# Attention with negated scores and one q stack for two heads; part of the weights' sums moved from attention into the recurrence and the gate units

## The chip, the cores and the metric

The kernel runs on one core of a Trainium2 chip. The metric is the device time of one execution in microseconds (us). Engines are named as in the profile: PE is TensorE (matmuls and transposes; PEld is its weight load), DVE is VectorE, ACT is ScalarE, POOL is GpSimd, SP is SyncE, which here issues nearly all DMAs.

## The reference

One layer of a streaming encoder: 1024 tokens, 1024 features, float32. With h = RMSNorm(x):

```
z = h @ w_in                      # q, f, i, g of the recurrence; q, k, v of attention; two gates
oa = hgrn2_mixer(...)             # 4 heads of 128, gated linear recurrence, chunks of 64
ob = band_attention(q, k, v, ...) # 8 heads of 64; a chunk of 64 sees itself and 8 chunks before it
x = x + (sigmoid(gate_a) * (oa @ w_branch_a) + sigmoid(gate_b) * (ob @ w_branch_b)) @ w_out
x = x + (silu(h2 @ w_gate) * (h2 @ w_up)) @ w_down          # h2 = RMSNorm(x), 2816 wide
x = x + sigmoid(h3 @ w_ple_gate) * (p @ w_ple_proj)         # h3 = RMSNorm(x)
```

The part that the change touches most is the band attention:

```
qh, kh = head_rms(q, qn_g), head_rms(k, kn_g)   # t * rsqrt(mean(t*t over the head) + 1e-6) * gain
scores = qh @ kh.T / 8 + rel_bias[clipped distance]   # -1e30 outside the band
o = softmax(scores) @ v
```

## The kernel before

**Matmuls.** Every matmul of weights is made of three: each operand is split into a rounded part hi and a rest lo, and hi*hi, hi*lo and lo*hi are summed in PSUM. The hi of a weight is cast by ACT (line 123) and its rest lo is subtracted by POOL, sometimes DVE (line 126). Weights pass through `weights()`: load by SP into `raw` (2 buffers), cast, rest, into a ring of 4, up to three units ahead of use. Large products (w_out, the gates, the feed-forward) use Strassen's scheme with 7 products in place of 8; the sums of weight blocks that it needs are S1 to S4.

**Who sets the order.** `Pinned` and `order()` chain PE's matmuls, SP's DMAs and the operations called through `self.V`, `self.A` and `self.G` in the order of the program text; their line in the profile is 54, since the helper records them. Other operations are placed by the framework's scheduler. The program is written as generators ("streams") that yield after a piece of PE work; `weave` interleaves two of them by their planned PE time, `drain` runs one to its end.

**Stages.** `first_norm` loads x and starts the first products. `hgrn_in(h)` projects head h of the recurrence; its inner part `near(h)` prepares products. `hgrn_mix(h)` runs the recurrence of a head by levels m = 1, 2, 4 .. 64: at each level DVE multiplies halves of q and kt (SBUF operands), PE makes the scores, and DVE puts them into place with `copy_predicated` under 0/1 `masks` (32-bit words, levels below 32). `hgrn_in(h+1)` is woven with `hgrn_mix(h)`, and `attn_v` with the last mix. Then come `attention()`, `gate_units()`, `branches()`, `out_proj()`, the feed-forward and the last part.

**Attention.** 32 steps, each one pair of heads and one block of 128 queries. `attn_in` (a feed taken piece by piece) makes q and k of four heads at a time; for the head norm ACT squares, DVE sums over 64, and POOL takes the power -1/2 (line 556) and multiplies by the token's factor r (line 557); `r64` = r*r/64 is made once on DVE (lines 526, 527). `attn_stack` transposes q and k of a pair into PSUM; ACT copies them with their gains into k1 and `qs` (two tiles of 128 columns), DVE makes the rests k2 and the lower half of qs. `attn_scores` multiplies, and one DVE operation per part adds the bias and keeps a running maximum; DVE negates the maximum, ACT takes exp with it as bias, and DVE or ACT divides by the row's sum (head 1: DVE's TENSOR_SCALAR over the row). `attn_pt` transposes the probabilities and copies them into `pt`, `attn_pv` multiplies with v.

**The weights' sums.** S1 to S4 of w_out (4 jobs) and of w_down (11 jobs) are worked out by POOL from the raw weights and spilled to DRAM until their stage. `quad_slow` does this: per job two loads of 512 KB, four POOL operations of 128x512 (lines 1069, 1073, 1075, 1080) and four stores, in four slots of the large pool. 12 jobs (`QUADS`) run beside attention, two stream steps for each of its yields, and the other 3 in `gate_units`, one step for each of the five later yields of `strassen_weights`, in all units but the last.

Of the kernel before, what the change touches and what calls it, by code (L numbers as in the profile page):

```python
# [9 lines left out]

F32 = mybir.dt.float32
F32R = mybir.dt.float32r
U32 = mybir.dt.uint32
AF = mybir.ActivationFunctionType
ALU = mybir.AluOpType
AX = mybir.AxisListType

P = 128
# [3 lines left out]
HALF = 512  # L22
# [9 lines left out]
RAW = 2  # L32
AHEAD = 3
PLAIN = 4
QUADS = 12


C_MIX, C_FFN, C_PLE, C_ON, C_GQ, C_GK, C_LB = 0, 8, 16, 24, 25, 26, 27
# [3 lines left out]
def f32(ap):  # L42
    return ap.bitcast(F32)
# [13 lines left out]
class Trunk:  # L57
# [150 lines left out]
    def norm_sums(self):  # L208

        nc = self.nc  # L210
        ps = self.mm()
        for b in range(8):
            self.mul(ps[:, b:b + 1], self.acc[:, b * P:b * P + P], self.ones[:, 0:1], start=True, stop=True)
        v = self.small(8)
        nc.vector.tensor_scalar(v, ps[:, 0:8], 1.0 / D, EPS, ALU.mult, ALU.add)
        self.r = self.small(8, tag="rtok")
        nc.gpsimd.tensor_tensor(self.r, v, self.mhalf[:, 0:8], ALU.pow)

    def norm_rows(self):

# [300 lines left out]
    def attn_in(self):  # L521

        nc = self.nc
        late = []
        self.r64 = self.small(8, tag="r64")
        nc.vector.tensor_tensor(self.r64, self.r, self.r, ALU.mult)
        nc.vector.tensor_scalar(self.r64, self.r64, 1.0 / 64, None, ALU.mult)

        def scale():
            two, b, ps, ss = late.pop(0)  # L530
            for i in range(2):
                qk = self.small(HALF, tag="qk")
                self.V.tensor_tensor(
                    qk[:, :].rearrange("p (a two d) -> p a two d", two=2, d=64),
                    ps[:, i * 256:i * 256 + 256].rearrange("p (a d) -> p a d", d=64).unsqueeze(2).to_broadcast([P, 4, 2, 64]),
                    ss[:, 4 * i:4 * i + 4].unsqueeze(2).unsqueeze(3).to_broadcast([P, 4, 2, 64]), ALU.mult)
                self.qk[2 * two + i, b] = qk

        for two in range(2):
            ws = self.weights(4, ahead=0)  # L540
            for b in range(8):
                pss = []
                for n, _ in enumerate(self.tokens(ws, (b,), pss)):
                    if b == 7:
# [12 lines left out]
                nc.gpsimd.tensor_scalar(ss, ss, self.r[:, b:b + 1], None, ALU.mult)  # L557
                late.append((two, b, ps, ss))
                yield 1296
        while late:  # L560
            scale()

    def attn_stack(self, pair, b):

        qk = self.qk.pop((pair, b))
        ps = self.mm()
        for a in range(4):
            self.tr(ps[:, a * P:a * P + P], qk[:, a * P:a * P + P], self.eye)
        t = slice(b * P, b * P + P)
# [4 lines left out]
        qsrc = [ps[:, h * P:h * P + P] for h in range(2)]  # L574
        for h in range(2):
            self.A.activation(k1[h][:, t], ksrc[h], AF.Copy, scale=gk)
            self.A.activation(qs[h], qsrc[h], AF.Copy, scale=self.gq8[:, 0:1])
        yield
        for h in range(2):
            self.V.scalar_tensor_tensor(k2[h][:, t], ksrc[h], gk, f32(k1[h][:, t]), ALU.mult, ALU.subtract)  # L580
            lo = qs[h][64:128, :]
            self.V.scalar_tensor_tensor(lo, qsrc[h][64:128, :], self.gq8[64:128, 0:1], f32(lo), ALU.mult, ALU.subtract)

    def attn_scores(self, pair, b, h):

        nb = min(b + 1, 5)
        cols = nb * P
        k0 = (b + 1 - nb) * P
        na = {1: 1, 2: 2, 3: 3, 4: 2, 5: 3}[nb] * P
        bias = self.bias[pair, h]  # L590
        q = self.qs[pair, b][h]
        k1, k2 = [k[pair % 2 * 2 + h] for k in (self.k1, self.k2)]
        s = self.small(640, tag="s")
        mx = self.small(2, tag="mx2")
        last = None
        for i, (lo, hi) in enumerate(((0, na), (na, cols))):
            if hi == lo:
                continue
            ps = self.mm()
            n = hi - lo  # L600
            self.mul(ps[:, :n], q, k1[:, k0 + lo:k0 + hi], start=True, stop=False)
            self.mul(ps[:, :n], q, k2[:, k0 + lo:k0 + hi], start=False, stop=True)
            init = -3.0e38 if last is None else last
            self.V.tensor_tensor_reduce(s[:, lo:hi], ps[:, :n], bias[:, 640 - cols + lo:640 - cols + hi], 1.0, init, ALU.add, ALU.max, mx[:, i:i + 1])
# [191 lines left out]
    def gate_units(self, sums):  # L796
# [42 lines left out]
        for n in range(units):  # L839

            def side():
# [206 lines left out]
    def quad_slow(self, jobs):  # L1048
# [18 lines left out]
        for n, (_, k, sums) in enumerate(jobs):  # L1067
# [760 lines left out]
    def run(self):  # L1828
# [18 lines left out]
        with ExitStack() as es:  # L1847
# [8 lines left out]
            self.r = self.rb = None  # L1856
            self.gates = []
            self.hg, self.ended, self.pend, self.qk, self.bias, self.ob = {}, [], [], {}, {}, []
            self.oa = [None] * 4
            with ExitStack() as mixer:  # L1860
                self.masks = mixer.enter_context(tc.tile_pool(name="levels", bufs=1)).tile([P, len(LEVELS), 64], U32, name="masks")
# [39 lines left out]
            drain(self.ple())  # L1901


SMALL = {"rb": 1, "rtok": 1, "r64": 1, "state": 1, "t8": 2, "t4": 4, "mx2": 4, "neg": 4, "den": 4}
QUARTERS = {"whiq": 3, "wloq": 3}
FFN = {"q1024": 1, "q512": 3, "raw": 2, "tmp": 8}
MIXER = {"s": 3, "pt": 3, "bias": 4, "qk": 4, "qs": 4, "sq": 1}


class Small:  # L1910
# [9 lines left out]
def drain(stream):  # L1920
    while True:
        try:
            next(stream)
        except StopIteration as e:
            return e.value


def weave(main, side, main_ns, side_ns):
# [56 lines left out]
def layout(i):  # L1985
# [37 lines left out]
    d["masks"] = np.stack(mk, axis=1).astype(np.uint32)  # L2023
    return {n: np.ascontiguousarray(v) for n, v in d.items()}


# [13 lines left out]
```

## Time and profile before

| what | value |
|---|---|
| median of 3 runs | 1595.65 us (1594.68 to 1601.39) |
| the profiled execution: its own time | 1595.63 us |
| its span, first to last instruction | 1593.7 us |
| granted TensorE clock | 0.998 |
| HBM read, written | 163.82 MB, 65.27 MB |
| q1 (the hardware queue of SP's DMAs): share of 16 engines' span | 40.6% |

The span is what the views divide; the time of the run is 1.9 us longer. An engine's busy time counts its instructions from start to end; a matmul's end is modelled, so a short wait of PE can look shorter than it was. In rows of groups, `out<-in` are tile names without their numbers, then partitions x elements and type, the count, the busy time in us and the mean in ns, then the idle time of the engine just before them with what ended it. In rows of the timeline the first number is the start in us, the second the duration, and brackets hold the idle time before it and its releaser.

### The profile page before, as it was taken

What the parts mean: (1) busy time and instruction counts of PE and PEld (TensorE: products, weight loads), DVE (VectorE), ACT (ScalarE), POOL (GpSimd) and SP (SyncE); (2) the same over time, 40 slices, a digit from 0 to 9 for tenths busy, and PEclk for the clock granted to TensorE, in tenths of its full rate; (3) what the DMA queues carried; (4) which work ended last, traced back from release to release, by engine and by line L of the source; (5) the groups of instructions that cost most, each with busy time, mean ns of one, the idle gap of its engine ahead of it and who ended that gap; (6) DMA issues with size and microseconds to landing.
All of it is one profiled execution on the core that took longest, in us unless ns stands there. A gap on an engine that the chain in (4) does not pass through costs nothing.

```text
span 1593.7 us, 21834 instructions
## 1 busy us (share of the span) xinstructions
PE 1566.2 (98%) x8224; PEld 1309.3 (82%) x8224; DVE 1171.8 (74%) x1767; ACT 643.7 (40%) x1089; POOL 783.6 (49%) x445
## 2 busy tenths in 40 slices
PE   8999999999999999999999999999999999999997
PEld 6998989877888888888887788888888888888886
DVE  5656765489998777544898988888888866765658
ACT  5321221167677633421377322232222234445453
POOL 3422221257563064325230777777777764644554
PEclk9999999999999999999999999999999999999999
DMA  5101100245663465475244422233333268875334
GB/s 191 54 28 41 40 28 27 100 146 174 224 245 107 143 192 187 146 285 210 80 141 177 152 99 99 100 99 109 103 108 108 80 255 322 304 278 189 126 134 157
DMA packets 81897, 230.52 MB, mean 145 GB/s; under 512 B 9216, under 2 KB 9984, under 8 KB 81280
## 3 DMA queue, kind: packets, MB, share of 16 engines
q1 hardware_dynamic: 81648, 229.12, 40.6%
q8 instruction: 64, 1.05, 0.2%
q14 instruction: 41, 0.34, 0.1%
q10 hardware_dynamic: 144, 0.02, 0.0%
HBM read 163.82 MB, written 65.27 MB: 144 GB/s over the span
## 4 chain that ended last, share of the span: by engine, by line
PE 80%; DVE 9%; POOL 2%; ACT 2%; issue 2%; DMA 1%; SPq 0%; POOLq 0%; ACTq 0%; DVEq 0%
PE pm L83 77%; DVE s L54 5%; PE pm L86 2%; DVE m L54 2%; ACT s L54 1%; POOL wl L126 1%; POOL m L556 1%; DVE q L54 0%; DVE wl L126 0%; ACT wh L123 0%; DVE pm L54 0%; DMA d<-s 0%; DMA s<-in_oq 0%; POOL s L1075 0%; DMA wr<-d 0%
## 5 line engine op out<-in xcount | busy, mean ns | idle before, releaser
L83 PE MATMUL pm<-s,wh 128*128 128x512 f32 (+1 forms) x1712 | 532.1, 392 | 6.7 <-ACT wh L123 5.2
L83 PE MATMUL pm<-s,whi 128*128 128x512 f32 x1568 | 488.1, 392 | 1.2 <-DVE t L54 1.2
L126 POOL TENSOR_TENSOR wl<-wr,wh 128x1024 fp32r<-128x1024 f32 (+2 forms) x108 | 265.0, 2460 | 395.9 <-ACT wh L123 392.6
L83 PEld LDWEIGHTS pm<-s,wh 128*128 128x128 f32 x1712 | 320.1, 189 | 73.7 <-ACT wh L123 5.2
L83 PEld LDWEIGHTS pm<-s,whi 128*128 128x128 f32 x1568 | 294.7, 188 | 67.0 <-DVE t L54 1.7
L83 PE MATMUL pm<-s,wl 128*128 128x512 f32 (+1 forms) x856 | 334.1, 390 | 0.0
L54 DVE TENSOR_TENSOR s<-s,s 128x512 f32<-128x512 f32 (+4 forms) x213 | 257.3, 1236 | 90.5 <-ACT s L54 53.1
L83 PE MATMUL pm<-s,wlo 128*128 128x512 f32 x784 | 307.9, 393 | 0.9 <-DVE wlo L54 0.5
L83 PE MATMUL pm<-wh,s 128*128 128x256 f32 (+1 forms) x896 | 238.2, 340 | 0.0
L123 ACT CAST wh<-wr 128x1024 fp32r<-128x1024 f32 (+2 forms) x114 | 114.8, 1008 | 268.5 <-PE pm L83 143.9
L83 PEld LDWEIGHTS pm<-s,wl 128*128 128x128 f32 x856 | 161.5, 189 | 34.2 <-POOL wl L126 0.6
L83 PEld LDWEIGHTS pm<-s,wlo 128*128 128x128 f32 x784 | 147.4, 188 | 35.0 <-DVE wlo L54 1.1
L83 PEld LDWEIGHTS pm<-wh,s 128*128 128x128 f32 x896 | 154.6, 190 | 13.9 <-DVE s L341 0.2
L54 DVE TENSOR_TENSOR t<-pm,t 128x512 f32<-128x512 f32 x138 | 94.8, 687 | 88.3 <-PE pm L83 81.9
L54 DVE TENSOR_TENSOR s<-pm,s 128x512 f32<-128x512 f32 (+1 forms) x134 | 87.0, 680 | 86.4 <-PE pm L83 86.2
L83 PE MATMUL pm<-wl,s 128*128 128x256 f32 (+1 forms) x448 | 147.5, 329 | 0.4 <-POOL wl L126 0.4
L54 POOL TENSOR_TENSOR wlo<-wr,whi 128x512 fp32r<-128x512 f32 (+1 forms) x53 | 107.5, 2037 | 74.9 <-ACT whi L54 74.1
L54 ACT CAST whi<-q 128x512 fp32r<-128x512 f32 (+1 forms) x81 | 61.4, 757 | 153.4 <-DVE q L54 131.3
L54 POOL TENSOR_TENSOR s<-s,t 128x512 f32<-128x512 f32 x44 | 76.8, 1745 | 86.7 <-ACT t L54 86.7
L54 ACT CAST s<-s 128x1024 fp32r<-128x1024 f32 (+1 forms) x94 | 90.2, 980 | 61.8 <-DVE s L54 31.9
L54 POOL TENSOR_TENSOR wlo<-q,whi 128x512 fp32r<-128x512 f32 x52 | 87.9, 1691 | 45.7 <-ACT whi L54 31.9
L83 PEld LDWEIGHTS pm<-wl,s 128*128 128x128 f32 x448 | 85.3, 191 | 5.9 <-POOL wl L126 0.6
(147 smaller groups left out, 1949.2 us busy)
## 6 DMA issues: line engine op xcount, KB each, us to landing
d<-s SPq DMA_DIRECT2D x147, 256.0 KB, 3.4
s<-d SPq DMA_DIRECT2D x67, 512.0 KB, 5.9
wr<-d SPq DMA_DIRECT2D x36, 512.0 KB, 4.0
s<-in_wq SPq DMA_DIRECT2D x22, 512.0 KB, 5.4
wr<-in_sg SPq DMA_DIRECT2D x22, 512.0 KB, 3.9
wr<-in_su SPq DMA_DIRECT2D x22, 512.0 KB, 3.8
s<-in_x SPq DMA_DIRECT2D x21, 512.0 KB, 8.0
d<-s SPq DMA_DIRECT2D x18, 512.0 KB, 6.1
```

Source lines behind the costliest of these rows:

```text
L54: return lambda *a, **k: self.trunk.order(op(*a, **k), self.key)
L83: return self.order(self.nc.tensor.matmul(*a, **k))
L86: return self.order(self.nc.tensor.transpose(*a, **k))
L123: self.nc.scalar.copy(hi[:, c], raw[:, c])
L126: rest.tensor_tensor(lo[:, c], raw[:, c], f32(hi[:, c]), ALU.subtract)
L556: nc.gpsimd.tensor_tensor(ss, ss, self.mhalf[:, 0:8], ALU.pow)
```

## The change

- Scores are kept negated: the score instruction multiplies by -1 and keeps a running minimum, which is at once the bias of exp(-s + min). The negation and its tile go.
- `qs` is one tile of 256 columns for both heads of a pair (2 buffers in place of 4 of half the size): one ACT copy and one DVE rest in place of two each.
- The head norm uses mean(t*t) + eps*v in place of mean(t*t)*r*r + eps, with v = 1/(r*r) of the token: its power -1/2 already holds the factor r. `epsv` = eps*v is made on DVE in `norm_sums` of the first norm; `r64` and POOL's multiplication go.
- `masks` are bytes. `pt` has 4 buffers in place of 3.
- 8 jobs of sums in place of 12 run early, and no longer in attention: `quad_early` cuts each job into two halves of 256 columns (`quad_piece`: one load of 512 KB, four POOL operations of 128x256, four stores of 128 KB) in two buffers of the pool `late1`, and `beside` advances them by one step at each yield of `hgrn_in` and `attn_v`. The other 7 jobs run in `gate_units`, one or two steps by turns at each later yield, now in the last unit too.

```diff
         self.r = self.small(8, tag="rtok")
         nc.gpsimd.tensor_tensor(self.r, v, self.mhalf[:, 0:8], ALU.pow)
+        if self.epsv is None:
+            self.epsv = self.small(8, tag="epsv")
+            nc.vector.tensor_scalar(self.epsv, v, EPS, None, ALU.mult)
...
-        self.r64 = self.small(8, tag="r64")
-        nc.vector.tensor_tensor(self.r64, self.r, self.r, ALU.mult)
-        nc.vector.tensor_scalar(self.r64, self.r64, 1.0 / 64, None, ALU.mult)
...
-                self.V.tensor_scalar(ss, ss, self.r64[:, b:b + 1], EPS, ALU.mult, ALU.add)
+                self.V.tensor_scalar(ss, ss, 1.0 / 64, self.epsv[:, b:b + 1], ALU.mult, ALU.add)
                 nc.gpsimd.tensor_tensor(ss, ss, self.mhalf[:, 0:8], ALU.pow)
-                nc.gpsimd.tensor_scalar(ss, ss, self.r[:, b:b + 1], None, ALU.mult)
...
-        qs = self.qs[pair, b] = [self.small(P, F32R, tag="qs") for _ in range(2)]
+        qs = self.small(256, F32R, tag="qs")
+        self.qs[pair, b] = [qs[:, h * P:h * P + P] for h in range(2)]
...
-            self.V.tensor_tensor_reduce(s[:, lo:hi], ps[:, :n], bias[:, ...], 1.0, init, ALU.add, ALU.max, mx[:, i:i + 1])
+            self.V.tensor_tensor_reduce(s[:, lo:hi], ps[:, :n], bias[:, ...], -1.0, init, ALU.add, ALU.min, mx[:, i:i + 1])
             last = mx[:, i:i + 1]
-        neg = self.small(1, tag="neg")
-        self.V.tensor_scalar(neg, last, -1.0, None, ALU.mult)
...
-        self.A.activation(s[:, :cols], s[:, :cols], AF.Exp, bias=neg, accum_out=den)
+        self.A.activation(s[:, :cols], s[:, :cols], AF.Exp, bias=last, scale=-1.0, accum_out=den)
...
-                for _ in more:
-                    if n + 1 < units:
+                for i, _ in enumerate(more):
+                    for _ in range(1 + i % 2):
                         next(sums, None)
                     yield
...
+    def quad_piece(self, src, k, sums, half):
+        G, cols = self.nc.gpsimd, HALF // 2
+        w = self.slot(late=True)
+        at = slice(half * cols, half * cols + cols)
+        self.load(w[:, :].rearrange("p (i c) -> p i c", i=4), src.rearrange("p (i c) -> p i c", i=4)[:, :, at])
+        for _ in range(5):
+            yield
+        a11, a21, a22, a12 = [w[:, i * cols:i * cols + cols] for i in range(4)]
+        for out, x, y, op in ((a22, a21, a22, ALU.add), (a21, a11, a21, ALU.subtract), (a11, a22, a11, ALU.subtract), (a12, a12, a11, ALU.subtract)):
+            G.tensor_tensor(out, x, y, op)
+            yield
+        yield
+        to = slice(k % 2 * HALF + at.start, k % 2 * HALF + at.stop)
+        for kind, part in zip(("S2", "S3", "S1", "S4"), (a11, a21, a22, a12)):
+            if k % 2 == 0 and half == 0:
+                sums[kind, k // 2] = self.spill()
+            self.store(sums[kind, k // 2][:, to], part)
...
+    def quad_early(self, jobs):
+        pieces = [self.quad_piece(*job, half) for job in jobs for half in range(2)]
+        live = []
+        while pieces or live:
+            if pieces:
+                live.append(pieces.pop(0))
+            for _ in range(6):
+                for x in list(live):
+                    if next(x, x) is x:
+                        live.remove(x)
+                yield
...
-                drain(self.hgrn_in(0, outs))
+                jobs = [(d["oq"][k], k, self.osums) for k in range(4)] + [(d["wq"][k], k, self.sums) for k in range(NFF // 2)]
+                sums = self.quad_early(jobs[:QUADS])
+                drain(beside(self.hgrn_in(0, outs), sums))
                 for h in range(3):
-                    weave(self.hgrn_in(h + 1), self.hgrn_mix(h), 41500, 17000)
+                    weave(beside(self.hgrn_in(h + 1), sums), self.hgrn_mix(h), 41500, 17000)
                 self.feed = self.attn_in()
-                weave(chain(self.attn_v(), islice(self.feed, FIRST)), self.hgrn_mix(3), 41500 + 1300 * FIRST, 17000)
+                weave(beside(chain(self.attn_v(), islice(self.feed, FIRST)), sums), self.hgrn_mix(3), 41500 + 1300 * FIRST, 17000)
+                drain(sums)
                 self.attn_setup()
-                jobs = [(d["oq"][k], k, self.osums) for k in range(4)] + [(d["wq"][k], k, self.sums) for k in range(NFF // 2)]
-                sums = self.quad_slow(jobs[:QUADS])
-                for n, _ in enumerate(self.attention()):
-                    for _ in range(2):
-                        if n > 1:
-                            next(sums, None)
-                drain(sums)
+                drain(self.attention())
```

More of the change, by code (lines that the diff above doesn't have):

```diff
@@ L12 @@
 F32R = mybir.dt.float32r
-U32 = mybir.dt.uint32
+U8 = mybir.dt.uint8
 AF = mybir.ActivationFunctionType
@@ L34 @@
 PLAIN = 4
-QUADS = 12
+QUADS = 8
 C_MIX, C_FFN, C_PLE, C_ON, C_GQ, C_GK, C_LB = 0, 8, 16, 24, 25, 26, 27
@@ L571, in attn_stack @@
         k1, k2 = [k[pair % 2 * 2:pair % 2 * 2 + 2] for k in (self.k1, self.k2)]
-        qs = self.qs[pair, b] = [self.small(P, F32R, tag="qs") for _ in range(2)]
+        qs = self.small(256, F32R, tag="qs")
+        self.qs[pair, b] = [qs[:, h * P:h * P + P] for h in range(2)]
         ksrc = [ps[:, 256 + h * P:256 + h * P + P] for h in range(2)]
[L574 to L577, printed above, removed]
+        qsrc = ps[:, 0:256]
+        self.A.activation(k1[0][:, t], ksrc[0], AF.Copy, scale=gk)
+        self.A.activation(qs, qsrc, AF.Copy, scale=self.gq8[:, 0:1])
+        self.A.activation(k1[1][:, t], ksrc[1], AF.Copy, scale=gk)
         yield
+        lo = qs[64:128, :]
         for h in range(2):
             self.V.scalar_tensor_tensor(k2[h][:, t], ksrc[h], gk, f32(k1[h][:, t]), ALU.mult, ALU.subtract)
-            lo = qs[h][64:128, :]
-            self.V.scalar_tensor_tensor(lo, qsrc[h][64:128, :], self.gq8[64:128, 0:1], f32(lo), ALU.mult, ALU.subtract)
+            if h == 0:
+                self.V.scalar_tensor_tensor(lo, qsrc[64:128, :], self.gq8[64:128, 0:1], f32(lo), ALU.mult, ALU.subtract)
     def attn_scores(self, pair, b, h):
@@ L602, in attn_scores @@
             self.mul(ps[:, :n], q, k2[:, k0 + lo:k0 + hi], start=False, stop=True)
-            init = -3.0e38 if last is None else last
-            self.V.tensor_tensor_reduce(s[:, lo:hi], ps[:, :n], bias[:, 640 - cols + lo:640 - cols + hi], 1.0, init, ALU.add, ALU.max, mx[:, i:i + 1])
+            init = 3.0e38 if last is None else last
+            self.V.tensor_tensor_reduce(s[:, lo:hi], ps[:, :n], bias[:, 640 - cols + lo:640 - cols + hi], -1.0, init, ALU.add, ALU.min, mx[:, i:i + 1])
             last = mx[:, i:i + 1]
-        neg = self.small(1, tag="neg")
-        self.V.tensor_scalar(neg, last, -1.0, None, ALU.mult)
         yield s, nb
         den = self.small(1, tag="den")
-        self.A.activation(s[:, :cols], s[:, :cols], AF.Exp, bias=neg, accum_out=den)
+        self.A.activation(s[:, :cols], s[:, :cols], AF.Exp, bias=last, scale=-1.0, accum_out=den)
         yield
@@ L1082, in quad_slow @@
         store(*prev)
+    def quad_piece(self, src, k, sums, half):
[16 more added lines that the diff above has]
+        yield
+        yield
+    def quad_early(self, jobs):
[8 more added lines that the diff above has]
+                        live.remove(x)
+                yield
     def quad_plan(self, plain, npairs, sums):
@@ L1855, in run @@
             self.setup()
-            self.r = self.rb = None
+            self.r = self.rb = self.epsv = None
             self.gates = []
@@ L1860, in run @@
             with ExitStack() as mixer:
-                self.masks = mixer.enter_context(tc.tile_pool(name="levels", bufs=1)).tile([P, len(LEVELS), 64], U32, name="masks")
+                self.masks = mixer.enter_context(tc.tile_pool(name="levels", bufs=1)).tile([P, len(LEVELS), 64], U8, name="masks")
                 outs = self.first_norm()
@@ L1901, in run @@
             drain(self.ple())
-SMALL = {"rb": 1, "rtok": 1, "r64": 1, "state": 1, "t8": 2, "t4": 4, "mx2": 4, "neg": 4, "den": 4}
+SMALL = {"rb": 1, "rtok": 1, "epsv": 1, "state": 1, "t8": 2, "t4": 4, "mx2": 4, "den": 4}
 QUARTERS = {"whiq": 3, "wloq": 3}
 FFN = {"q1024": 1, "q512": 3, "raw": 2, "tmp": 8}
-MIXER = {"s": 3, "pt": 3, "bias": 4, "qk": 4, "qs": 4, "sq": 1}
+MIXER = {"s": 3, "pt": 4, "bias": 4, "qk": 4, "qs": 2, "sq": 1}
 class Small:
@@ L1925, in drain, with beside @@
             return e.value
+def beside(main, side):
+    for x in main:
+        next(side, None)
+        yield x
 def weave(main, side, main_ns, side_ns):
@@ L2022, in layout @@
         mk.append(s // m == t // m - 1)
-    d["masks"] = np.stack(mk, axis=1).astype(np.uint32)
+    d["masks"] = np.stack(mk, axis=1).astype(np.uint8)
     return {n: np.ascontiguousarray(v) for n, v in d.items()}
```

## The prediction

> **What bounds the kernel now.** I read the page first: its first part for the busiest engine, its fourth for the chain of work that ended last.
>
> ```profile
> span 1593.7 us, 21834 instructions
> ...
> PE 1566.2 (98%) x8224; PEld 1309.3 (82%) x8224; DVE 1171.8 (74%) x1767; ACT 643.7 (40%) x1089; POOL 783.6 (49%) x445
> ...
> PE 80%; DVE 9%; POOL 2%; ACT 2%; issue 2%; DMA 1%; SPq 0%; POOLq 0%; ACTq 0%; DVEq 0%
> ```
>
> TensorE (PE) is busy 98% of the span: 1593.7 - 1566.2 = 27.5 us are not PE's. In the changed build the matmuls are the same and stand in the same order on PE, so the change can only take away or add waits of PE. The next question is in which stage those waits lie. The busy times by stretch, cut at the stages (36 to 318 us: recurrence and attn_v; 318 to 528: attention; 528 to 677: gate units; then the rest), tell that. Columns: the stretch, its length, busy time and count for PE, PEld, DVE, ACT, POOL, then granted clock, DMA share and rate.
>
> ```profile
> core 0: us, PE busy (x) PEld busy (x) DVE busy (x) ACT busy (x) POOL busy (x), PEclk, DMA share, GB/s
> 36.00:318.00 282.00, 280.07 (x2000) 253.86 (x2000) 165.07 (x334) 59.52 (x102) 75.59 (x40) 1.00 0.13 47
> 318.00:528.00 210.00, 204.61 (x1462) 168.75 (x1461) 181.41 (x608) 149.76 (x410) 113.49 (x89) 1.00 0.50 170
> 528.00:677.00 149.00, 149.00 (x665) 121.81 (x664) 106.31 (x128) 64.14 (x94) 59.48 (x35) 1.00 0.52 178
> 677.00:1594.00 917.00, 903.69 (x3993) 742.72 (x3991) 696.01 (x675) 346.95 (x459) 522.43 (x271) 1.00 0.45 162
> ```
>
> PE stands idle 1.9 us in the recurrence, 5.4 us in attention (210.00 - 204.61), nothing in the gate units. In attention DVE is busy 181.4 of 210 us (86%), in the recurrence 165 of 282 (59%). So the most that the lighter attention can give is about 5.4 us, plus what the modelled ends of matmuls hide of each wait. That is 0.34% of the time: a change of attention's second engine in a kernel that is PE's. The waits of PE in attention, and then those in the recurrence (in total, times, longest):
>
> ```profile
> PE pm L86 <- DVE m L54: 4.0, 6, 1.3
> PE pm L83 <- DVE m L54: 1.1, 2, 0.8
> ```
>
> ```profile
> PE pm L83 <- DVE s L54: 1.4, 3, 0.5
> ```
>
> All are waits for DVE. No wait for a weight's rest (wl) or for a DMA is among those of either stage. The timeline shows what DVE did before the large ones:
>
> ```profile
> 367.22 1.27 POOL L1073 TENSOR_TENSOR s<-s 128x512 f32<-128x512 f32 x1
> 367.53 1.25 DVE L54 TENSOR_SCALAR m<-m,m 128x512 f32<-128x512 f32 x1
> 368.93 0.71 PE L86 MATMUL pm<-eye,m 128*128 128x128 f32 x4 [1.00 <-DVE m L54]
> ...
> 375.02 1.60 DVE L54 TENSOR_SCALAR m<-m,m 128x640 f32<-128x640 f32 x1
> 376.68 0.77 PE L86 MATMUL pm<-eye,m 128*128 128x128 f32 x5 [1.03 <-DVE m L54]
> ...
> 394.82 2.38 POOL L126 TENSOR_TENSOR wl<-wr,wh 128x1024 fp32r<-128x1024 f32 x1 [1.54 <-ACT wh L123]
> 396.00 1.24 DVE L54 TENSOR_SCALAR m<-m,m 128x8 f32<-128x8 f32 x1
> 397.62 0.85 PE L83 MATMUL pm<-s,m 128*128 128x384 f32 x4 [0.85 <-DVE m L54]
> ...
> 497.07 1.29 DVE L54 TENSOR_TENSOR m<-pm,m 128x512 f32<-128x512 f32 x2 [1.15 <-POOL m L557]
> 498.42 0.44 PE L86 MATMUL pm<-eye,m 128*128 128x128 f32 x2 [1.31 <-DVE m L54]
> ```
>
> The softmax scale (TENSOR_SCALAR of a whole score row) is stretched while POOL works on a weight sum (L1073), and the transposes that need it come 1.00 and 1.03 us late. At 396 an operation of 8 columns takes 1.24 us beside a weight's rest on POOL. At 497 DVE waits for POOL's last step of the q/k norm. These four make 4.2 of the 5.4 us; the other 1.2 us are small waits, most in the first steps.
>
> **The change in attention.** Groups of this stage (count, busy us, mean ns, idle before):
>
> ```profile
> L54 ACT ACTIVATE m<-pm,gq 128x128 fp32r<-128x128 f32 x64 | 23.6, 368 | 0.0
> L54 DVE SCALAR_TENSOR_TENSOR m<-pm,gq,m 64x128 fp32r<-64x128 f32 x64 | 22.9, 357 | 0.9
> L1073 POOL TENSOR_TENSOR s<-s 128x512 f32<-128x512 f32 x12 | 15.6, 1299 | 0.9
> L54 DVE TENSOR_SCALAR m<-m 128x1 f32<-128x1 f32 x64 | 9.8, 154 | 2.2
> L557 POOL TENSOR_SCALAR m<-m,m 128x8 f32<-128x8 f32 x16 | 5.0, 313 | 1.3
> ```
>
> - The 64 negations go: 64 x 0.154 = 9.8 us of DVE, two in each of 32 steps, and each stood between the scores and their exponential.
> - The 64 residues of q (357 ns) become 32 of twice the columns. One costs between 0.36 and 0.71 us, so DVE saves 0 to 11.4 us; I take the middle, 6. The 64 copies of q on ACT (368 ns) likewise give 0 to 11.8 us on an engine that is busy 150 of 210 us: off the path, nothing.
> - 12 jobs of 4 POOL sums leave, 48 x 1.3 = 62 us of POOL's 113.5, and the 16 multiplications at L557 (0.31 us each), which stood at the end of the chain that DVE awaited at 497. A third buffer more for pt, and scale -1 with a minimum in the same score instruction, cost nothing.
>
> DVE thus loses 9.8 + 6 = 16 of 181 us, 0.5 us a step, and its whole-row operations no longer meet the sums. The waits at 369 and 377 should go whole (2.0 us). The one at 398 goes if DVE comes early enough (its POOL neighbour is a weight's rest, which stays). That at 498 goes in good part: the multiplication (0.31) and the DVE lead (0.5) are taken off 1.31. Of the 1.2 us of small ones perhaps half. That is 2.0 + 0.85 + 0.8 + 0.6 = 4.3 us of the visible idle time. A matmul's modelled end reaches over the start of each wait, so the true waits are longer than shown, by an amount that no row gives; I take the whole visible 5.4 us as gain, with 2 us (the two sure ones) and 8 us (half as much again) as its ends.
>
> **The change in the recurrence.** 8 jobs are cut in two: 16 loads, 64 POOL operations of 128x256 and 64 stores go beside hgrn_in and attn_v. The rows of the stage and what a meeting with POOL looks like there:
>
> ```profile
> L54 DVE TENSOR_TENSOR s<-s,s 128x512 f32<-128x512 f32 x56 | 43.5, 817 | 32.7 <-PE pm L83 32.7
> L54 DVE COPY_PREDICATED s<-masks,pm 128x512 f32<-128x512 uint32 x20 | 18.9, 945 | 0.0
> ```
>
> ```profile
> L126 POOL TENSOR_TENSOR wl<-wr,wh 128x1024 fp32r<-128x1024 f32 x20 | 48.1, 2414 | 144.5 <-ACT wh L123 142.4 <-issue 1.3 <-POOL wl L126 0.8
> ```
>
> ```profile
> 155.36 3.51 DVE L54 TENSOR_TENSOR s<-s,s 128x512 f32<-128x512 f32 x2
> 155.67 2.64 POOL L126 TENSOR_TENSOR wl<-wr,wh 128x1024 fp32r<-128x1024 f32 x1 [12.58 <-ACT wh L123]
> 158.92 1.15 PE L83 MATMUL pm<-s,s 128*64 128x64 f32 x16 [0.54 <-DVE s L54]
> ```
>
> A pair of DVE products that takes 2 x 0.82 = 1.6 us on the mean took 3.5 us, until POOL's operation was done; PE paid 0.54 of the 1.9 us lost, some 0.29. An operation of 256 columns, worked out from 2414 ns for 1024 and 1299 for 512 (1115 per 512), is about 0.74 us, so the sums bring 64 x 0.74 = 47 us of POOL, 17% of the stage; they end by attn_v, so I take 20%. Of the 56 products some 20% meet one in progress and wait half of it: 56 x 0.2 x 0.37 = 4.1 us of DVE, of which PE at 0.29 pays 1.2 us. With smaller products, and the masks' first two levels, I take +1.5 us. The ends are 0 (all hidden: DVE idles 41% of the stage) and 64 x 0.74 = 47 us (PE pays every one).
>
> Here a rule of the Trainium skill speaks against the move (SBUF — State Buffer, section on the two separate sides): a port pair is shared by VectorE and GpSimd as an exclusive lock, taken by a VectorE operation with two SBUF inputs (or in a two-port mode) or by a GpSimd one, and the loser blocks until the whole instruction is over. By this rule the move takes the sums from a stage whose DVE reads mostly PSUM to one whose level products all read two SBUF inputs; the trace agrees at 155.36. If PE paid all 4.1 us of such blocking, the sum would be 1594.3.
>
> - The masks as bytes in place of 32-bit words: no byte mask is in the trace. 20 operations of 945 ns; between half and double that, -9 to +19 us of DVE, at 0.29 for PE -2.7 to +5.5. The same elements go through, so I take 0.
> - SP's queue: the stores wait for POOL, and weight loads stand behind them in order. Cover: PE waits for no weight in this stage (the waits above are DVE's), and DMA is at a share of 0.13. Without that cover a late load costs one piece's POOL time, 4 x 0.74 = 3 us.
> - In the first norm epsv takes the place of a small step that attention's norm had: 0.
>
> **The change in the gate units.** 7 jobs in place of 3 run there, up to 7 operations a unit. POOL's rows of a unit without them:
>
> ```profile
> 631.82 1.29 POOL L54 TENSOR_TENSOR wlo<-q,whi 128x512 fp32r<-128x512 f32 x1 [6.22 <-DVE t L54]
> 639.36 1.29 POOL L54 TENSOR_TENSOR wlo<-q,whi 128x512 fp32r<-128x512 f32 x1 [6.25 <-ACT whi L54]
> ```
>
> Two gaps of 6.2 us hold 12.5 us; 7 x 1.3 = 9.1 us fit. PE was never idle here, also while units with 5 operations ran. I take 0; if POOL overflows, the four added jobs' 16 x 1.3 = 21 us bound it, and only what is beyond the gaps is paid.
>
> **Sum**, against the profiled execution's own 1595.63 us (span 1593.7 and 1.9 around it; the median of the runs is 1595.65, the same): 1595.63 - 5.4 + 1.5 + 0 = 1591.7 us.
>
> **Rivals.** *No net change*: attention's waits are the length of its chains, not the load. The wait at 498 speaks for it (DVE itself stood idle before it). Then only the two met sums are won, 2.0 us, and the recurrence takes 2 to 4: about 1596. Chance 0.22.
>
> *Slower: the lock in the recurrence*. PE's order is fixed there, and a level's products stand straight before the matmuls that need them, as at 158.92. Four sums of a piece may run back to back and catch product after product. From 5.4 / 0.74 = 8 operations paid in full on, the gain is gone; from (5.4 + 8) / 0.74 = 19 of 64 on, the kernel is slower by over 0.5%. At 24 of 64: 1595.6 - 5.4 + 17.8 = 1608. For it: the case at 155. Against it: at present 20 operations three times as long (2.4 us) leave PE only 1.4 us of waits for DVE. Chance 0.09.
>
> *More than forecast*: all of attention's waits go, hidden parts too, and the recurrence's slack takes the rest: 1595.6 - 8 = 1587.6. Chance 0.10. *The gate units overflow* by a few us: 1594 to 1597; chance 0.05.
>
> **How the numbers follow.** The forecast, 1591.7, has the other 0.54; by its ends (a gain of 3.5 to 6.5, a cost of 0.5 to 3) it is 1589.5 to 1595. About 0.5% (8 us) is what a measurement of this kernel can tell from no change; the forecast is within it. Faster by over 0.5% needs all of the greater gain: half of that rival and a little, 0.06. Slower: 0.09. Between: 0.85. The range takes in the forecast, the even case and part of both tails: 1587.5 to 1599.
>
> **What would show it.** Right: in attention, PE's idle time falls from 5.4 us to under 2, whole-row scales are no longer stretched, DVE's busy time is down by some 16 us; in the recurrence POOL is up by about 47 us, the level products' mean rises above 817 ns, PE's wait for DVE from 1.4 us to about 3; the gate units keep PE at 149 of 149. Wrong: PE's waits in attention stay (chains), the recurrence's rise past 7 us (lock), or a wait for wlo or wl appears.

## The result and the profile after

The changed kernel takes 1590.42 us (median of 14 runs, 1587.86 to 1593.77) against 1595.45 us before (14 runs, 1593.27 to 1601.39): a ratio of 0.9965, 95% interval 0.9958 to 0.9973. Forecast were 1591.7 us and a range of 1587.5 to 1599. The total came out as forecast, but two of the terms behind it did not: a loss was taken too small, and a gain of about its size was not foreseen. That the two nearly cancel is luck.

The page of the changed kernel, its first lines:

```profile
span 1585.9 us, 21744 instructions
...
PE 1559.4 (98%) x8224; PEld 1311.1 (83%) x8224; DVE 1166.6 (74%) x1670; ACT 639.8 (40%) x1057; POOL 802.0 (51%) x461
```

PE's own busy time has fallen by 6.8 us (1566.2 before), with the same 8224 matmuls in the same order; the idle time, 1585.9 - 1559.4 = 26.5 us, by 1.0 only. That is not what the prediction said: it let PE's waits alone change. The same stretches as before:

```profile
36.00:318.00 282.00, 276.33 (x1965) 250.28 (x1965) 171.34 (x326) 58.34 (x100) 128.24 (x103) 0.99 0.31 101
318.00:528.00 210.00, 208.09 (x1495) 173.43 (x1494) 160.26 (x518) 146.86 (x379) 48.49 (x27) 1.00 0.17 58
528.00:677.00 149.00, 149.00 (x672) 123.05 (x671) 115.27 (x131) 64.82 (x95) 87.13 (x51) 1.00 0.70 239
677.00:1594.00 917.00, 896.94 (x3986) 742.26 (x3984) 696.75 (x672) 346.37 (x458) 525.57 (x271) 0.99 0.47 161
```

PE's idle time in the recurrence went from 1.93 to 5.67 us, in attention from 5.39 to 1.91. In the gate units it is zero as before, but 672 matmuls now stand in the same 149 us in place of 665. The waits of PE, first the recurrence (without a single one of 0.3 us for `state`), then attention (without one of 0.2 us; the gate units have none):

```profile
PE pm L83 <- ACT s L447: 3.2, 2, 1.8
PE pm L83 <- DVE s L54: 1.3, 3, 0.5
PE pm L86 <- DVE s L54: 0.8, 1, 0.8
```

```profile
PE pm L83 <- DVE state L54: 1.0, 1, 1.0
PE pm L83 <- DVE m L54: 0.8, 2, 0.5
```

Half of what is left in attention is the first row, a wait for the last step of the recurrence. The four large waits for DVE, 0.85 to 1.31 us each, are gone. Groups of DVE in attention, the first of the kernel before, the others after:

```profile
L54 DVE TENSOR_SCALAR m<-m,m 128x512 f32<-128x512 f32 x4 | 3.8, 940 | 0.1
```

```profile
L54 DVE TENSOR_SCALAR m<-m,m 128x512 f32<-128x512 f32 x4 | 1.9, 488 | 0.1
L54 DVE SCALAR_TENSOR_TENSOR m<-pm,gq,m 64x256 fp32r<-64x256 f32 x32 | 15.7, 491 | 0.5
```

The whole-row scale takes about half as long, with no sum beside it. The residue of two q stacks costs 491 ns against 2 x 357.

In the recurrence, DVE's and POOL's groups after, with one of DVE before ahead of them:

```profile
L54 DVE TENSOR_TENSOR m<-s,s 128x512 f32<-128x512 f32 x12 | 8.7, 750 | 0.0
```

```profile
L54 DVE TENSOR_TENSOR s<-s,s 128x512 f32<-128x512 f32 x56 | 46.4, 868 | 29.4 <-PE pm L83 29.3
L54 DVE COPY_PREDICATED s<-masks,pm 128x512 f32<-128x512 uint8 x20 | 18.8, 940 | 0.0
L54 DVE TENSOR_TENSOR m<-s,s 128x512 f32<-128x512 f32 x12 | 11.0, 946 | 0.0
L1093 POOL TENSOR_TENSOR s<-s 128x256 f32<-128x256 f32 x64 | 55.8, 873 | 52.4 <-DMA s<-in_wq 24.4 <-DMA s<-in_oq 21.4 <-DMA d<-s 2.9
```

DVE's products of two SBUF operands of 512 columns became longer beside the sums (817 to 868 ns, 750 to 946 ns); the masked copy, which reads PSUM, did not (945 to 940 ns; bytes in place of words cost and bring nothing).

Idle time is not all that a stage loses. The matmuls are the same in the same order, so their starts can be compared one by one. Those that start from 36.05 to 318.10 us before, 282.0 us in all, start from 35.81 to 324.66 us after; those of attention, 210.0 us before, take from there to 528.20. These two stretches of the changed kernel, and one inside the first:

```profile
35.81:324.66 288.85, 282.22 (x2001) 255.33 (x1999) 173.59 (x333) 59.69 (x103) 130.37 (x104) 0.99 0.32 104
324.66:528.20 203.54, 202.59 (x1461) 168.74 (x1460) 158.21 (x512) 145.91 (x379) 46.36 (x25) 1.00 0.15 51
173.74:177.14 3.40, 3.40 (x19) 3.40 (x18) 0.56 (x2) 0.23 (x1) 0.69 (x1) 0.50 0.02 5
```

For the same matmuls the recurrence takes 6.8 us longer and attention 6.5 us less. Of the 6.8 us, 4.7 are idle time (6.6 us in place of 1.9; the wait of 1.0 us for `state` is among these matmuls). Some 1.7 us more are in the third row: right behind the wait of 1.8 us, which ended at 173.26, the granted clock was 0.50 for 3.4 us. In the profiled execution of before the granted clock was 1.00 all through this stage. So far the recurrence lost about what attention won. What is left is in code that the change did not touch. The Strassen matmuls of the gate units and the feed-forward, before and then after, each as one group of the whole span and as the stretch from 1000 to 1200 us, where PE never waits:

```profile
L83 PE MATMUL pm<-s,whi 128*128 128x512 f32 x1568 | 488.1, 392 | 1.2 <-DVE t L54 1.2
```

```profile
1000.00:1200.00 200.00, 200.00 (x871) 163.48 (x870) 172.80 (x162) 55.33 (x82) 149.40 (x84) 1.00 0.32 105
```

```profile
L83 PE MATMUL pm<-s,whi 128*128 128x512 f32 x1568 | 483.0, 389 | 0.6 <-DVE t L54 0.6
```

```profile
1000.00:1200.00 200.00, 200.00 (x884) 165.64 (x883) 178.18 (x163) 58.71 (x86) 152.39 (x87) 1.00 0.32 103
```

200 us hold 871 matmuls before (229.6 ns each) and 884 after (226.2 ns), 1.5% more, at a granted clock of 1.00 both times. PE's busy share can't show that: it is 100% in both. A count of matmuls in a fixed window does. Before, they are not all slower; two windows of 4 us from the kernel before, 1103.5 to 1107.7 and 1107.8 to 1112.3:

```profile
L83 PE MATMUL pm<-s,whi 128*128 128x512 f32 x14 | 4.3, 389 | 0.0
...
L83 PE MATMUL pm<-s,whi 128*128 128x512 f32 x14 | 4.5, 394 | 0.0
```

Slow and normal stretches of some 4 us take turns there, in a regular pattern. The program says which is which. Of the seven products of a Strassen unit, numbers 0, 3 and 6 take their weights from `whi` and `wlo` tiles of 512 columns; the other four take halves of tiles of 1024 columns, from the ring that all weights pass through. With the trace's matmuls set against the program's order, the next matmul starts 232 ns after one on a tile of 512 columns in the kernel before, and 227 ns after one on the ring (medians). In the changed kernel it is 227 ns for both.

One thing did change for the tiles of 512 columns: they lie behind the pool `neg`, the ring lies ahead of it. Each of the four `neg` tiles takes 32 bytes of a partition, so without them all that is allocated behind lies 128 bytes lower. The first `whi` of 512 columns lay at 179840 (128 past a multiple of 256), and now lies at 179712 (a multiple of 512). The ring's first `whi` lies at 18944 in both kernels, also a multiple of 512.

### The profile page after: what moved, and what is told of

It is laid out like the page before. It is cut to its first block, busy times and chain, and to the rows that moved or that the text cites. A ratio compares the mean times of both kernels' runs of the same rounds, so it can differ in the third digit from the quotient of the medians.

```text
span 1585.9 us, 21744 instructions
## 1 busy us (share of the span) xinstructions
PE 1559.4 (98%) x8224; PEld 1311.1 (83%) x8224; DVE 1166.6 (74%) x1670; ACT 639.8 (40%) x1057; POOL 802.0 (51%) x461
## 4 chain that ended last, share of the span: by engine, by line
PE 80%; DVE 6%; DMA 6%; POOL 4%; issue 2%; ACT 2%; SPq 1%; POOLq 0%; ACTq 0%; DVEq 0%
PE pm L83 77%; DVE s L54 3%; PE pm L86 3%; POOL wl L126 2%; DMA d<-s 1%; POOL s L1093 1%; DMA s<-in_oq 1%; DMA wr<-d 1%; DVE m L54 1%; SPq L78 1%; DMA wr<-in_qk 1%; DVE q L54 0%; POOL s L54 0%; ACT wh L123 0%; DMA wr<-in_fm 0%
## 5 line engine op out<-in xcount | busy, mean ns | idle before, releaser
L83 PE MATMUL pm<-s,whi 128*128 128x512 f32 x1568 | 483.0, 389 | 0.6 <-DVE t L54 0.6
L126 POOL TENSOR_TENSOR wl<-wr,wh 128x1024 fp32r<-128x1024 f32 (+2 forms) x108 | 269.5, 2500 | 321.1 <-ACT wh L123 314.9
```

What stands on the lines that cost most here:

```text
L83: return self.order(self.nc.tensor.matmul(*a, **k))
L126: rest.tensor_tensor(lo[:, c], raw[:, c], f32(hi[:, c]), ALU.subtract)
```

## The experiments

**Two that move addresses alone.** In e1 the kernel before gets the changed kernel's addresses for the tiles of the Strassen stages:

```
-        mx = self.small(2, tag="mx2")
+        mx = self.small(3, tag="mx2")
...
-        neg = self.small(1, tag="neg")
+        neg = mx[:, 2:3]
...
-SMALL = {..., "mx2": 4, "neg": 4, "den": 4}
+SMALL = {..., "mx2": 4, "den": 4}
```

> The kernel before with one edit: the negated maximum is kept in a third column of the maximum's tile, so that the pool neg goes and every tile that is laid out behind the small pools (the Strassen stages' whi, wlo, q, wr, t among them) lies 128 bytes lower, where the changed kernel has them. Theory address: the Strassen matmuls pm<-s,whi fall from a mean of 392 to 389 ns, as in the changed kernel, and the time is 1595.5 - 7.9 = 1587.6 us. Rival (the faster matmuls come from what runs beside them, thus from the moved sums): the mean stays 392 ns and the time 1595.5, within 1 us.

Measured: 1588.06 us against 1595.78, ratio 0.9949 (0.9935 to 0.9964).

```profile
L83 PE MATMUL pm<-s,whi 128*128 128x512 f32 x1568 | 483.2, 389 | 1.3 <-DVE t L54 1.3
```

In e2 the changed kernel gets the addresses of before:

```
+            self.tp.tile([P, 32], F32, "pad", "pad")
             self.setup()
...
+SMALL = {..., "den": 4, "pad": 1}
```

> The changed kernel with one edit: an unused tile of 128 bytes behind the small pools, so that the late tiles lie where the kernel before had them. Theory address: the mean of pm<-s,whi goes from 389 to 392 ns and the time to 1590.4 + 7.9 = 1598.3 us, slower than before the change. Rival: 389 ns and 1590.4 us, within 1 us.

Measured: 1598.25 us, ratio to before 1.0013 (0.9999 to 1.0026).

```profile
L83 PE MATMUL pm<-s,whi 128*128 128x512 f32 x1568 | 488.1, 392 | 1.2 <-DVE t L54 1.2
```

The same 389 and 392 ns both ways: 128 bytes are worth 7.7 us in the one (1595.78 - 1588.06) and 7.8 in the other (1598.25 - 1590.42). And e2 says what the change is worth without them: 2.5 us on the wrong side (1598.25 - 1595.78), with an interval that just takes in no difference.

**Where the recurrence lost.** e3 leaves POOL's four operations out of each early piece (the sums of 8 jobs are left out); loads and stores stay.

```
         for out, x, y, op in (...):
-            G.tensor_tensor(out, x, y, op)
             yield
```

> The changed kernel without the four POOL operations of each early piece (the pieces are loaded and stored as they are, so the sums of 8 jobs are left out). Theory POOL beside DVE (the two block each other in the recurrence): the idle time of PE from 36 to 318 us falls from 5.7 us to about 2, the level products' mean to about 817 ns, and the time to about 1586. Rival, SP's queue (stores wait for POOL there and weight loads stand behind them): also falls, as no store waits for POOL any more, but then DVE's products are not shorter. Rival, DMA traffic: idle time stays above 5 us, 1590 us.

Measured: 1585.38 us, ratio 0.9925 (0.9910 to 0.9940); against the changed kernel 5.0 us less. The recurrence of e3:

```profile
36.00:318.00 282.00, 278.79 (x1982) 253.05 (x1982) 162.79 (x332) 58.08 (x99) 75.58 (x40) 0.99 0.33 106
```

Idle time of PE in the recurrence is 3.2 us, of which 1.4 is one wait for `state`, which stayed with the pieces' DMAs (below). The level products are back at 816 ns on the mean. So most of the loss comes from POOL's operations, as the first theory had it. How they reach PE is seen in the timeline ahead of the 1.8 us wait for ACT's copy, DVE and POOL after, then DVE's same operations in e3:

```profile
156.73 1.84 DVE L54 TENSOR_TENSOR s<-s,s 128x512 f32<-128x512 f32 x2
157.98 2.82 POOL L126 TENSOR_TENSOR wl<-wr,wh 128x1024 fp32r<-128x1024 f32 x1
158.49 2.60 DVE L323 TENSOR_SCALAR s<-s,lb,lb 128x512 f32<-128x512 f32 x1
...
161.01 4.25 POOL L1093 TENSOR_TENSOR s<-s 128x256 f32<-128x256 f32 x4 [0.21 <-DMA s<-in_wq]
...
162.65 2.01 DVE L54 TENSOR_TENSOR m<-s,s 128x512 f32<-128x512 f32 x2
164.58 2.92 DVE L54 TENSOR_TENSOR s<-s,s 128x512 f32<-128x512 f32 x2
...
170.85 0.96 DVE L54 TENSOR_TENSOR m<-s,s 128x512 f32<-128x512 f32 x1
```

```profile
155.80 3.50 DVE L54 TENSOR_TENSOR s<-s,s 128x512 f32<-128x512 f32 x2
159.22 0.53 DVE L323 TENSOR_SCALAR s<-s,lb,lb 128x512 f32<-128x512 f32 x1
...
161.31 1.28 DVE L54 TENSOR_TENSOR m<-s,s 128x512 f32<-128x512 f32 x2
162.52 2.39 DVE L54 TENSOR_TENSOR s<-s,s 128x512 f32<-128x512 f32 x2
...
168.26 0.67 DVE L54 TENSOR_TENSOR m<-s,s 128x512 f32<-128x512 f32 x1
```

From the first of these to the end of the last, DVE takes 15.1 us after (156.73 to 171.81) and 13.1 in e3 (155.80 to 168.93), 2.0 us more. ACT casts what the last product made and then, in its order, copies the scores that PE waits for (L447); that wait is 1.76 us after and 0.20 in e3. Each kernel has one long meeting with a weight's rest (L126): after, four sums stood ahead of the rest in POOL's order, so it came 1.9 us later and met the scale at L323 (2.60 us in place of 0.53) and not the pair of products (3.50 us in e3). The 2.0 us come from the products that follow: POOL worked on four sums back to back (161.01 to 165.26), and then on L369, which stood behind them.

Before the change the same wait for ACT's copy (there line 444) was small, the second of two rows for the recurrence:

```profile
PE pm L83 <- ACT s L444: 0.4, 2, 0.2
```

**The sums back in attention.** e4 is the changed kernel with its 8 early jobs run as whole jobs in attention.

```
-                sums = self.quad_early(jobs[:QUADS])
...
-                drain(self.attention())
+                sums = self.quad_slow(jobs[:QUADS])
+                for n, _ in enumerate(self.attention()):
+                    for _ in range(1 + n % 2):
+                        if n > 1:
+                            next(sums, None)
+                drain(sums)
```

> The changed kernel, with its 8 early jobs of sums back in attention, whole (loads of 512 KB, POOL operations of 512 columns) by one or two steps for each yield; nothing of them in the recurrence. Theory (the recurrence lost what it lost to these sums; the lighter attention has room for them): PE idle 36 to 318 us back to 2, attention's idle time 2 to 4 us in place of 1.9, so 1590.4 - 3.7 + 1 = about 1587. Rival (attention's waits come from the sums on POOL, not from DVE's load): attention's idle time back to 5.4 us or more, and the time 1590 or more.

Measured: 1583.23 us, ratio 0.9922 (0.9907 to 0.9937), 7.2 us below the changed kernel: this version beats both. That is 4 us less than expected, since the expectation took the recurrence's loss to be its idle time alone.

```profile
36.00:318.00 282.00, 280.13 (x1998) 253.89 (x1998) 163.94 (x335) 59.63 (x102) 75.97 (x41) 1.00 0.14 47
318.00:528.00 210.00, 208.49 (x1500) 173.33 (x1499) 164.63 (x517) 149.02 (x381) 87.43 (x57) 1.00 0.41 137
```

The recurrence is back at 1.9 us of idle time, and attention has 1.5 with the sums in it. e8 goes the rest of the way back, with `QUADS = 12` and two steps at each yield:

> Made from e4, with 12 jobs in attention at two steps for each yield, as in the kernel before; the gate units have 3. Theory (attention's waits went because DVE has less to do there): attention's idle time stays at 1.5 to 3 us, time 1583 to 1585. Rival (they went because fewer sums run, so later and further apart): idle time 4 to 5.4 us, time 1586 to 1588.

Measured: 1585.25 us, ratio 0.9933 (0.9918 to 0.9948).

```profile
318.00:528.00 210.00, 207.69 (x1496) 172.25 (x1495) 168.25 (x517) 147.68 (x381) 108.77 (x73) 1.00 0.52 175
```

2.3 us of idle time with all 12 jobs where the kernel before had 5.4: the other edits of attention did that, not the sums' absence. The whole-row scale of 512 columns is stretched again (854 ns on the mean, 940 before), and PE does not pay for it as it did. In time e8 is 2.8 us below e1, which has the same addresses of the Strassen tiles and the old attention; their intervals overlap, and so do those of e8 and e4. Which of the edits counts was not tried apart.

**Which tiles.** e5 and e6 split the 128 bytes, starting from e4: in e5 `whi` and `wlo` lie 128 higher and the other tiles of the stage 512 higher, in e6 the other tiles lie 128 higher and `whi`, `wlo` stay.

> Made from e4. whi and wlo of the Strassen stages lie 128 bytes higher (where the kernel before had them, 128 past a multiple of 512), while q, wr and t of these stages lie 512 higher, so at the same remainder as in e4. Theory (PE's own reads of a weight tile off a multiple of 512 are slower): pm<-s,whi at 392 ns, time 1583.2 + 7.9 = 1591. Rival (writes and reads of the other engines and DMAs in q, wr and t at an odd place take SBUF time from PE): 389 ns and 1583.

> Made from e4, the other half: q, wr and t of the Strassen stages 128 bytes higher, whi and wlo where e4 has them. Theory (PE's own reads): 389 ns and 1583. Rival (the other engines' tiles): 392 ns and 1591.

Measured: e5 1591.37 us, ratio 0.9973 (0.9958 to 0.9987); e6 1584.82, ratio 0.9918 (0.9901 to 0.9934). The group in e5, then in e6:

```profile
L83 PE MATMUL pm<-s,whi 128*128 128x512 f32 x1568 | 488.3, 393 | 0.4 <-DVE t L54 0.4
```

```profile
L83 PE MATMUL pm<-s,whi 128*128 128x512 f32 x1568 | 483.1, 389 | 1.3 <-DVE t L54 1.3
```

It is the weights' own tiles. e7, e11 and e12 move all late tiles of e4 by 256, 64 and 192 bytes (the pad of e2 in that size).

> Made from e4, with 256 bytes behind the small pools: every late tile lies 256 past a multiple of 512. If a multiple of 256 is enough: 389 ns and 1583. If it takes a multiple of 512: 391 to 394 ns and 1589 to 1592.

> Made from e4, with 64 bytes behind the small pools: late tiles 64 past a multiple of 256. If any place off a multiple of 256 is slow: pm<-s,whi at 392 ns and about 1591 us. If only the place at 128 is: 389 ns and 1583.

> Made from e4, with 192 bytes behind the small pools: late tiles 192 past a multiple of 256. Same two readings: 392 ns and about 1591 us, or 389 ns and 1583.

Measured: e7 1582.83 us, e11 1591.07 us, e12 1586.24 us. Matmuls in the same stretch, in that order:

```profile
1000.00:1200.00 200.00, 200.00 (x884) 165.62 (x883) 176.69 (x163) 57.19 (x83) 152.40 (x87) 1.00 0.30 99
```

```profile
1000.00:1200.00 200.00, 200.00 (x871) 163.28 (x870) 173.58 (x160) 58.20 (x86) 149.81 (x85) 1.00 0.31 100
```

```profile
1000.00:1200.00 200.00, 200.00 (x880) 165.03 (x879) 177.12 (x163) 57.35 (x84) 151.90 (x86) 1.00 0.30 99
```

A multiple of 256 is enough; 64 and 128 past it cost the whole 13 matmuls, 192 past it a third of them, which neither reading had. At 192 the matmuls on `whi` alone are slower (391 ns on the mean), those on `wlo` are not (389).

**Two that missed.** e9 cuts each early POOL operation into two of 128 columns.

```
-            G.tensor_tensor(out, x, y, op)
+            for c in range(0, cols, 128):
+                G.tensor_tensor(out[:, c:c + 128], x[:, c:c + 128], y[:, c:c + 128], op)
```

> The changed kernel with each early POOL operation of 256 columns cut into two of 128 (128 operations in place of 64, the same elements). Theory block (a DVE operation with two SBUF inputs waits until the POOL operation in progress is over, so shorter ones let it in sooner): DVE's products m<-s,s fall from 946 ns toward 850, PE's idle time from 36 to 318 us from 5.7 to 4 or less, time about 1588.5. Rival (the sums' work as a whole takes the share from DVE, however it is cut; more operations have more fixed cost): 946 ns or more, idle time 5.7 or more, time 1590 to 1592.

Measured: 1589.17 us, ratio to before 0.9960 (0.9946 to 0.9973), not to be told from the changed kernel's 0.9965. Of its recurrence a group of DVE and the stretch:

```profile
L54 DVE TENSOR_TENSOR s<-s,s 128x512 f32<-128x512 f32 x56 | 42.1, 792 | 32.0 <-PE pm L83 32.0
```

```profile
36.00:318.00 282.00, 275.27 (x1956) 250.20 (x1955) 161.75 (x325) 57.94 (x99) 138.32 (x167) 0.99 0.31 99
```

DVE's level products became shorter (868 to 792 ns), and its busy time in the stage fell from 171.34 to 161.75 us. The Trainium skill (SBUF — State Buffer, section "SBUF: two separate sides") has the loser blocked until the other's whole instruction is over; shorter instructions that free DVE agree with that. The products m<-s,s fell only from 946 to 918 ns, not toward 850. PE did not gain: one wait of 3.7 us for `state` took the place of others (idle time 6.7 us), so neither reading came out whole, and DVE's blocking alone is not the recurrence's loss. The timeline shows what set that wait. POOL had to wait for a piece's load and then worked on eight halves from 120.81 to 124.16 us; behind them in its order stood the small power (L477, until 125.15), which DVE awaited for 7.0 us before it could get to `state` at 126.22.

e10 has POOL issue the early stores in place of SP.

```
-            self.store(sums[kind, k // 2][:, to], part)
+            self.order(G.dma_start(sums[kind, k // 2][:, to], part), "poolq")
```

> The changed kernel with the early pieces' stores issued by POOL in place of SP, so that no weight load stands behind a store that waits for a sum. Theory queue (the wait of PE for state at 321 us, 1.0 us, comes from a weight load late behind the stores): that wait goes, the waits for ACT's copy (3.2 us) stay, time about 1589.4. Rival (SP's queue costs nothing; issuing takes POOL's time): the wait at 321 stays and time is 1590.4 or more.

Measured: 1599.28 us, ratio 1.0023 (1.0014 to 1.0032). The wait for `state` at attention's start is what it was to take away. In the changed kernel it looks so in the timeline:

```profile
315.65 1.05 ACT L123 CAST wh<-wr 128x1024 fp32r<-128x1024 f32 x1 [1.70 <-DMA wr<-in_qk]
...
316.77 2.39 POOL L126 TENSOR_TENSOR wl<-wr,wh 128x1024 fp32r<-128x1024 f32 x1 [2.17 <-ACT wh L123]
...
319.12 1.01 POOL L477 TENSOR_TENSOR m<-m,mhalf 128x4 f32<-128x4 f32 x1
...
321.60 0.49 PE L83 MATMUL pm<-state,s 128*128 128x128 f32 x2 [0.96 <-DVE state L54]
```

ACT waits for a weight load, POOL's rest comes late by that, and behind it in POOL's order the power that DVE needs before it gets to `state`. e3, with the stores, has this wait; e4, without them, and e10 have none in this place: it goes with the stores on SP. The waits for ACT's copy did not stay; in their place PE waits 4.9 us for `state` and 6.0 us for `s`, both from DVE, in the recurrence. The issuing cost far more than it saved:

```profile
L1100 POOL DMA_DIRECT2D d<-s x64 | 35.2, 556 | 0.0
...
L54 DVE TENSOR_TENSOR m<-s,s 128x512 f32<-128x512 f32 x12 | 19.1, 1616 | 0.0
```

64 issues held POOL for 35 us, and the products m<-s,s took 1616 ns in place of 946. PE's idle time from 36 to 318 us is 10.9 us and the granted clock of the stage 0.98, with three stretches of 3.4 us at 0.50 behind waits of 1.8 to 3.4 us.

## Why the prediction was right in its total and wrong in two terms

The steps in time, from medians: before to e1 (addresses) -7.7; e1 to e8 (lighter attention) -2.8; e8 to e4 (8 jobs there, not 12) -2.0; e4 to the changed kernel (8 jobs to the recurrence) +7.2. Together -5.3, and -5.0 measured. The middle two are each within what their intervals leave open. Matmul by matmul, the two profiled executions say the same: recurrence +6.8, attention -6.5, gate units and all behind them -8.1 us (their times are 7.4 us apart, 1595.63 and 1588.19).

- **Attention, -5.4**: right in size. Idle time fell by 3.5 us, by 4.4 without the wait inherited from the recurrence, and the stage takes 6.5 us less. DVE's busy time fell by 21 us (16 forecast for the lighter work; its rows give 17.0, the negations' 9.8 and 7.2 of the residues of q). The reason was right in part: e8 shows that the waits go also with all the sums beside attention, so meeting the sums does not by itself make them. The rival *No net change* said that the waits would stay, and they did not. Whether the load of DVE or the length of the chain made them is not shown, since the edits shorten the chain too.
- **Recurrence, +1.5**: the term that was mis-sized; it measured +7.2. The failed step is the count of what meets POOL and of what PE pays. It took a fifth of the 56 level products at half a wait each, and let PE pay 0.29 of that. The products m<-s,s were stretched as well; they stand in a chain that ends in ACT's copy, and PE's wait for that went from 0.4 to 3.2 us. The prediction said that all waits of this stage are for DVE; it showed one row of two, and left out this one. The sums' price was also low, 47 us against 55.8: most cost the 740 ns of the estimate (the median), but the mean is 873 since POOL is held up too. And no term was there for what a wait costs beyond its length, the 1.7 us at half the granted clock. By its idle time, 3.7 us, the sign for the lock (a rise past 7 us) did not show; by time the loss stands at it.
- **SP's queue, 0**: wrong by 1.0 us, the wait for `state`. Its cover, "PE waits for no weight", was true and not enough: a late weight load delayed POOL's rest, and with it a small POOL operation behind it in order.
- **The rival of the lock** thus was right in its mechanism in part and wrong in its price: more than the 5.4 us at which it said the gain is gone, far from the 17.8 it had at 24 paid sums. Four sums did run back to back and catch product after product, as it said; e9 shows that POOL's own order delays PE as well.
- **Gate units, 0 for the added jobs**: right; no wait of PE there with 7 jobs.
- **"The change can only take away or add waits of PE"**: wrong. The matmuls' own rate changed through the place of their weights, -7.7 us, more than the whole net gain. With the old addresses (e2) the change comes to +2.5 us: the gain that the forecast's terms add up to is not there, and the total was met by luck.

What stays open: whether it is PE's reading of weights off a multiple of 256 that is slow or the writing of ACT, DVE and POOL into them, since e5 moved both; and why 192 bytes past it slow `whi` alone. The granted clock's part is read from one profiled execution of each kernel.

## What to carry to other kernels

Compare counts of matmuls in a window where PE never waits before explaining a small change of time: a removed 32-byte tile can shift everything behind it. Compare the starts of the same matmuls in both traces to see what a stage lost; idle time alone showed 3.7 of 6.8 us here. Place weight tiles at a multiple of 256 bytes and hold them there while other edits are judged. When work is moved beside another stage, follow every chain there to PE, over DVE, ACT and POOL's own order, not only the operations that PE waits for today.

## What the runs showed of the hardware that was not expected

- With the weight tiles of 512 columns 64 or 128 bytes past a multiple of 256, 871 matmuls stand in 200 us in place of 884 (1.5%), at 192 bytes past it 880 (0.5%); at 256, nothing is lost. A matmul on such a tile is followed by the next after 232 ns in place of 227 (128 bytes, medians).
- A POOL operation of 256 columns with two SBUF operands took 740 ns at the median and 1842 at most beside DVE. In halves it was 574 ns each on the mean, so two halves cost a third more than the mean of 873.
- Issuing a DMA from POOL held that engine for 556 ns, and DVE's products m<-s,s with two SBUF inputs rose to 1616 ns in that kernel; the level products rose less (868 to 889 ns).
- From 45 to 528 us, each of the nine waits of PE of 1.5 us or more in the traces (the changed kernel, e1, e2, e9, e10) comes with 3.4 us at a granted clock of 0.50, which start at most 1.9 us after its end; the waits of 1.46 us and less there do not. Near 1500 us eight of ten such long waits do not either, and near 865 us the clock falls in several kernels with no wait over 0.6 us, so a wait's length alone does not decide it.
